# Regrouping HGRN2's short matrix products between the dense projections

## The chip, the core and the metric

The kernel runs on one core of one Trainium2 chip. The core's engines work beside each other, each on its own list of instructions in its own order: TensorE (PE in the profile; PEld is its loading of weights) multiplies matrices into the PSUM banks, VectorE (DVE) and ScalarE (ACT) do elementwise work, GpSimd (POOL) here mostly issues transfers, and SyncE (SP) issues the other transfers. Semaphores order work between engines. The metric is the device time of one execution in microseconds, lower is better. The median of three runs is 1842.91 us.

## The reference

A decoder trunk of two layers over 512 tokens and 1024 channels in float32. Each layer adds a half-step SwiGLU feed-forward, then three token mixers that share one normalised input and one output projection, then a second feed-forward. The part that matters is the HGRN2 mixer, a gated linear recurrence with 4 heads of 64 channels, computed in chunks of 64 tokens:

```python
bcum = jnp.cumsum(lfb, axis=-2)                       # lfb: log of the forget gate
rel = bcum[..., :, None, :] - bcum[..., None, :, :]
decay = jnp.where(causal, jnp.exp(jnp.where(causal, rel, 0.0)), 0.0)
scores = jnp.einsum('bhtd,bhsd,bhtsd->bhts', qb, kb, decay)
o = (jnp.einsum('bhts,bhsv->bhtv', scores, vb)
     + jnp.einsum('bhtd,bhdv->bhtv', qb * jnp.exp(bcum), state))
```

The decay depends on query token, key token and channel, so the scores of a chunk aren't one matrix product.

## The kernel before

The weights are streamed from memory. Each float32 weight tile is split into a high and a low part (a cast by ACT at line 301, a subtraction by DVE at line 302, into one of three `hl` buffers), and a dense product is three TensorE matmuls, high by high, high by low and low by high (lines 312, 318, 319). Python generators mix two kinds of work; the order in which they are recorded, turned into a list for each engine by a scheduler that knows their dependencies, is the order of execution on each engine.

In a layer's mixer stage `hgrn` (from line 1183 on) is such a generator, and the six dense projections of the attention group, `fox_qkv` (query, key and value of two halves, four steps each) are the other. After each part `hgrn` yields a number, and `mix` then records that many dense steps:

```python
for n in self.hgrn(l, hp, z, q, v, sg, og):
    for _ in range(n):
        next(dense, None)
```

One dense step is two weight tiles by four groups of 128 tokens by three matmuls: 24 matmuls of 128x256, all on TensorE. The 24 steps stand in the yields 1, 2, 4, 5, 5, 3, 3 and 1. A projection writes two PSUM banks, which ACT squares (line 1430), DVE reduces (line 1431) and DVE at last scales into the tile `qk` (line 1439) for the queries and keys; the value projections are split by lines 1447 and 1448. A later projection takes these banks again.

Between the dense steps `hgrn` puts bursts of short products, 64 rows by 64 columns of the array with 1, 32 or 64 columns moving through:

- line 1264: 32 products of keys and values, what each chunk adds to the recurrent state. ACT copies them out (line 1275), and DVE's scan over the chunks (line 1282) makes the states `S`.
- `scores` (line 1245): the scores in levels. A pair of query and key tokens belongs to the level of the highest bit in which their places in the chunk differ. For level l with half-width w = 2^(l-1), DVE makes the tile `e` from two half-width operations (lines 1332 and 1333), ACT takes its exponential, DVE multiplies its second halves by q into `e2` (line 1335), and 32 products of `e` and `e2` follow, 64x32 each. The diagonal (tile `e0`) and level 1 (tile `e1`) need only a sum over channels: 32 products each with a column of ones, one column wide.
- DVE writes each level into the score tile `A`: the diagonal at line 1287 by a multiplication, level 1 at line 1290 and the others at line 1344 by masked copies.
- `states` (line 1307): 28 products of `S` and the decayed queries, which ACT copies into `os` (lines 1315 and 1319).
- line 1360: 32 products of `A` and the values, the output.

Each of these float32 products shows as two matmul records in the profile, each with its own load of weights. The diagonal's and level 1's sums share two PSUM banks of tag `pt`; the levels' pairs take `pt`, `sc` and `pt` in turn; `states`, line 1264 and line 1360 take `sc`. Before the change the bursts of a layer are:

| burst | products | records | dense steps behind it |
|---|---|---|---|
| 1 | line 1264, sums of level 1, sums of the diagonal | 192 | 4 |
| 2 | levels 3 and 2, states | 184 | 5 |
| 3 | levels 5 and 4 | 128 | 5 |
| 4 | level 6 | 64 | 3 |
| 5 | output (line 1360) | 64 | 3 |

Of the kernel before, what the change touches and what calls it, by code (L numbers as in the profile page):

```python
# [23 lines left out]
P = 128  # L24
# [20 lines left out]
CH = 64  # L45
# [111 lines left out]
class Trunk:  # L157
# [1025 lines left out]
    def hgrn(self, l, hp, z, q, v, sg, og):  # L1183
        nc = self.nc
# [11 lines left out]
        h, t, n = tmp(), tmp(), tmp()  # L1196
# [44 lines left out]
        def scores(bank, at, held, moving, n):  # L1241
            for x in range(8):
                for hh, par in quarters:
                    c = 2 * x + par
                    nc.tensor.matmul(
                        bank[hh][rows[par], at + x * n : at + (x + 1) * n],
                        held[rows[hh], c * CH : (c + 1) * CH], moving(rows[hh], c),
                        start=True, stop=True,
                    )

        A = own("A", [P, 2, 8, CH])
        half = lambda a, w, i: a.rearrange("p (n two w) -> p n two w", two=2, w=w)[:, :, i, :]
        e0, e1 = tmp(), tmp()
# [6 lines left out]
        for x in range(8):  # L1260
            r, i = divmod(x, 4)
# [5 lines left out]
                    v[rows[par], i, f], start=True, stop=True,  # L1267
                )
        sb = [self.bank("pt") for _ in range(2)]
        for at, e in ((8, e1), (0, e0)):  # L1270
            scores(sb, at, e, lambda r, c: self.ones_c[r, :], 1)
        U, dec, S = tmp(), tmp(), own("S", [P, 2, HD, NCH])
        vc = lambda a: a.rearrange("p (r v c) -> p r v c", r=2, c=NCH)
        for par in range(2):
# [3 lines left out]
        for r in range(2):  # L1278
# [3 lines left out]
        nc.vector.tensor_tensor_scan(  # L1282
            S.rearrange("p r v c -> p (r v c)"), dec, U, 0.0, op0=ALU.mult, op1=ALU.add
        )
        for hh in range(2):
            d = lambda at, n: sb[hh][:, at : at + 8].unsqueeze(2).to_broadcast([P, 8, n])
            nc.vector.tensor_mul(
                A[:, hh], self.ident2.unsqueeze(1).to_broadcast([P, 8, CH]), d(0, CH)
            )
            nc.vector.copy_predicated(  # L1290
                A[:, hh, :, 1::2],
                self.lmask[:, 0, 1::2].unsqueeze(1).to_broadcast([P, 8, CH // 2]), d(8, CH // 2),
            )
        yield 4

# [4 lines left out]
        def states():  # L1300
            ob = [self.bank("sc") for _ in range(2)]
            for x in range(8):
                r, i = divmod(x, 4)
                for hh, par in quarters:
                    c = 2 * i + par
                    if c:
                        nc.tensor.matmul(
                            ob[hh][rows[par], x * CH : (x + 1) * CH], S[rows[hh], r, :, c - 1],
                            span(qe, r)[rows[hh], c * CH : (c + 1) * CH], start=True, stop=True,
                        )  # L1310
            for hh in range(2):
                for par in range(2):
                    out, src = chunk(os[rows[hh], :], par), C(ob[hh][rows[par], :])
                    if par:
                        nc.scalar.copy(out, src)
                    else:
                        for r in range(2):
                            x = slice(4 * r + 1, 4 * r + 4)
                            nc.scalar.copy(out[:, x, :], src[:, x, :])

        for group, then in (((2, 3), 5), ((4, 5), 5), ((6,), 3)):
            sb = [self.bank("pt" if group[0] != 4 else "sc") for _ in range(2)]
            made = []
            for at, lev in enumerate(group):
                w = 2**lev // 2
                e, e2 = tmp(), hp.tile([P, T], F32, tag=self.tt, name=self.n("e2"), bufs=self.tb)
                made.append((256 * at, lev, w, e, e2))
                n2 = W // (2 * w)
                ref = b.rearrange("p (n s) -> p n s", s=2 * w)[:, :, w - 1 : w].to_broadcast(
                    [P, n2, w]  # L1330
                )
                nc.vector.tensor_add(half(e, w, 0), half(kb, w, 0), ref)
                nc.vector.tensor_sub(half(e, w, 1), half(b, w, 1), ref)
                self.act(e, e, AF.Exp)
                nc.vector.tensor_mul(
                    e2.rearrange("p (n w) -> p n w", w=w), half(e, w, 1), half(q, w, 1)
                )
            for at, lev, w, e, e2 in made[::-1]:
                scores(sb, at, e, lambda r, c: e2[r, 32 * c : 32 * c + 32], 32)
            if group[0] == 2:  # L1340
                states()
            for at, lev, w, e, e2 in made[::-1]:
                for hh in range(2):
                    nc.vector.copy_predicated(
                        half(A[:, hh].rearrange("p x t -> p (x t)"), w, 1).rearrange(
                            "p (g n) w -> p g n w", g=8
                        ),
                        half(self.lmask[:, lev - 1, :], w, 1).unsqueeze(1).to_broadcast(
                            [P, 8, 32 // w, w]
                        ),  # L1350
                        sb[hh][:, at : at + 256].rearrange("p (g n w) -> p g n w", g=8, w=w),
                    )
            yield then

        ob = [self.bank("sc") for _ in range(2)]
        for x in range(8):
            r, i = divmod(x, 4)
# [6 lines left out]
        o, sq, r, t = tmp(), tmp(), tmp(), tmp()  # L1364
# [293 lines left out]
```

## Time and profile before

| | |
|---|---|
| median of three runs | 1842.91 us (1841.59 to 1846.96) |
| the profiled execution | 1837.37 us |
| its span, first to last instruction | 1835.6 us |
| PE, PEld, DVE, ACT, POOL busy | 99%, 92%, 79%, 54%, 9% |
| granted TensorE clock | 1.00 |
| the stage of bursts and dense steps, first layer | 401.5 to 481 us of the span |
| the same, second layer | 1306.9 to 1383 us |

All durations come from the one profiled execution, which was 5.5 us shorter than the median of the runs. An instruction's row has its start, its duration, the engine, the line of the kernel, what it writes and reads, its shape, and in brackets how long its engine stood idle before it and for what; "issue" means that the profile shows nothing it waited for. The ends of matmuls are modelled, and matmuls overlap: their starts tell the pace. An engine that is idle costs time only where PE comes to wait for it.

### The profile page before, as it was taken

How to read it: one execution, taken by the hardware profiler on the slowest of the kernel's cores; microseconds unless marked ns; L12 is line 12 of the kernel's file. 1: busy time of each engine (PE TensorE's matmuls, PEld its weight loads, DVE VectorE, ACT ScalarE, POOL GpSimd, SP SyncE). 2: the span in 40 equal slices, each digit the busy share in tenths (PEclk: the TensorE clock that was granted, in tenths of full speed). 3: DMA queues.
4: the chain of work that ended last, by engine and by line, in shares of the span. 5: the costliest groups of instructions: out<-in, count | busy, mean ns of one | idle time of the engine just before them, and what ended most of it. 6: DMA issues, size and time to landing. Idle time of an engine off the chain costs nothing.

```text
span 1835.6 us, 34734 instructions
## 1 busy us (share of the span) xinstructions
PE 1815.1 (99%) x14328; PEld 1685.2 (92%) x14328; DVE 1459.1 (79%) x2007; ACT 991.8 (54%) x1403; POOL 169.1 (9%) x168
## 2 busy tenths in 40 slices
PE   8999999999999999999999999999999999999999
PEld 6899999899878899999989999998997788999997
DVE  7888887676797888879668887875858878888883
ACT  4455555454675464555445555555547665555552
POOL 0011120100000001112001111201000000020210
PEclk9999999999999999999999999999999999999999
DMA  7659684232322766868266687813233228677762
GB/s 206 169 115 199 172 173 105 75 82 82 87 75 88 216 142 159 183 174 173 70 181 153 159 186 201 167 65 82 76 86 83 76 92 230 160 151 195 152 137 92
DMA packets 244782, 250.94 MB, mean 137 GB/s; under 512 B 19440, under 2 KB 229872, under 8 KB 244624
## 3 DMA queue, kind: packets, MB, share of 16 engines
q1 hardware_dynamic: 191024, 182.64, 32.5%
q0 software_dynamic: 53600, 66.09, 22.3%
q8 instruction: 112, 1.84, 0.4%
q14 instruction: 46, 0.38, 0.1%
HBM read 223.98 MB, written 2.10 MB: 123 GB/s over the span
## 4 chain that ended last, share of the span: by engine, by line
PE 89%; DVE 5%; ACT 3%; issue 1%; DMA 1%; SPq 1%; ACTq 0%
PE mm L312 13%; PE mm L319 13%; PE mm L318 13%; PE sc L319 6%; PE sc L318 6%; PE sc L312 6%; PE pt L312 6%; PE pt L318 6%; PE pt L319 6%; PE po L312 4%; PE po L318 4%; PE po L319 4%; DVE hl L302 1%; PE po L1510 1%; ACT hl L301 1%
## 5 line engine op out<-in xcount | busy, mean ns | idle before, releaser
L771 ACT CAST hl<-w 128x1024 fp32r<-128x1024 f32 x322 | 337.1, 1049 | 321.8 <-PE mm L319 79.0
L773 DVE TENSOR_TENSOR hl<-w,hl 128x1024 fp32r<-128x1024 f32 x322 | 392.8, 1222 | 86.8 <-ACT hl L771 86.6
L302 DVE TENSOR_TENSOR hl<-st,hl 128x512 fp32r<-128x512 f32 (+2 forms) x196 | 166.6, 853 | 119.3 <-ACT hl L301 118.0
L301 ACT CAST hl<-st 128x512 fp32r<-128x512 f32 (+2 forms) x196 | 146.4, 750 | 206.7 <-PE po L319 83.6
L312 PE MATMUL mm<-xc,hl 128*128 128x256 f32 (+1 forms) x732 | 201.5, 276 | 0.5 <-ACT g L882 0.5
L319 PE MATMUL mm<-xc,hl 128*128 128x256 f32 x728 | 201.4, 277 | 0.0
L318 PE MATMUL mm<-xc,hl 128*128 128x256 f32 x728 | 201.4, 277 | 0.0
L319 PE MATMUL sc<-xc,hl 128*128 128x256 f32 x528 | 146.6, 278 | 0.0
L312 PE MATMUL sc<-xc,hl 128*128 128x256 f32 (+1 forms) x530 | 146.6, 277 | 0.0
L318 PE MATMUL sc<-xc,hl 128*128 128x256 f32 x528 | 146.4, 277 | 0.0
L312 PEld LDWEIGHTS mm<-xc,hl 128*128 128x128 f32 x732 | 137.4, 188 | 0.9 <-ACT g L882 0.7
L319 PEld LDWEIGHTS mm<-xc,hl 128*128 128x128 f32 x728 | 136.7, 188 | 0.1
L318 PEld LDWEIGHTS mm<-xc,hl 128*128 128x128 f32 x728 | 136.7, 188 | 0.0
L312 PE MATMUL pt<-xc,hl 128*128 128x256 f32 (+1 forms) x484 | 133.4, 277 | 0.0
L318 PE MATMUL pt<-xc,hl 128*128 128x256 f32 x480 | 133.3, 278 | 0.0
L319 PE MATMUL pt<-xc,hl 128*128 128x256 f32 x480 | 133.0, 277 | 0.0
L312 PE MATMUL mm<-x,hl 128*128 128x512 f32 x272 | 108.9, 401 | 0.8 <-ACT cy L1158 0.8
L319 PE MATMUL mm<-x,hl 128*128 128x512 f32 x272 | 107.6, 395 | 0.0
L318 PE MATMUL mm<-x,hl 128*128 128x512 f32 x272 | 106.7, 392 | 0.0
L318 PEld LDWEIGHTS sc<-xc,hl 128*128 128x128 f32 x528 | 99.6, 189 | 0.0
L312 PEld LDWEIGHTS sc<-xc,hl 128*128 128x128 f32 x530 | 99.5, 188 | 0.2
L319 PEld LDWEIGHTS sc<-xc,hl 128*128 128x128 f32 x528 | 99.1, 188 | 0.1
(485 smaller groups left out, 5611.9 us busy)
## 6 DMA issues: line engine op xcount, KB each, us to landing
w<-in_ffn_w_in_dram SPq DMA_DIRECT2D x140, 512.0 KB
w<-in_ffn_w_out_dram SPq DMA_DIRECT2D x64, 512.0 KB
w<-in_ffn_w_out_dram POOLq DMA_DIRECT2D x56, 512.0 KB, 8.9
st<-in_w_mix_in_dram SPq DMA_DIRECT2D x88, 256.0 KB
st<-in_ffn_w_in_dram SPq DMA_DIRECT2D x72, 256.0 KB
w<-in_ffn_w_in_dram POOLq DMA_DIRECT2D x35, 512.0 KB, 8.4
w<-S POOLq DMA_DIRECT2D x35, 512.0 KB, 4.6
st<-in_ffn_w_out_dram SPq DMA_DIRECT2D x24, 512.0 KB
```

The costliest lines, as they stand in the source:

```text
L301: a = nc.scalar.copy(hi, src[:, c : c + w])
L302: b = nc.vector.tensor_sub(lo, src[:, c : c + w], hi)
L312: i = nc.tensor.matmul(acc[:, c], ah, bh[:, c], start=first and c.start == 0, stop=False, skip_group_check=True,)
L318: nc.tensor.matmul(acc, ah, bl, start=False, stop=False, skip_group_check=True)
L319: i = nc.tensor.matmul(acc, al, bh, start=False, stop=last, skip_group_check=True)
L771: A(nc.scalar.copy(hi, src))
L773: return lambda: V(nc.vector.tensor_sub(lo, src, hi))
L1510: nc.tensor.matmul(self.ob[:, t0 + u * P : t0 + 2 * P], V[:, j, h % 4].rearrange("p a d -> p (a d)"), part[:, j, u:, :].rearrange("p i t - ...
```

## The change

The 316 short products of a layer stay, and so do the 24 dense steps; their order changes. Level 1's sums move out of the first burst and follow level 2's products, into the same two banks (columns 256 to 263), and the masked copy of level 1 into `A` moves behind them. Levels 3 and 4 share a burst (banks `sc`), level 5 shares one with the states' products, level 6 stays alone. The yields become 1, 2, 4, 4, 4, 3, 2, 3 and 1, again 24.

| burst | products | records | dense steps behind it |
|---|---|---|---|
| 1 | line 1264, sums of the diagonal | 128 | 4 |
| 2 | level 2, sums of level 1 | 128 | 4 |
| 3 | levels 4 and 3 | 128 | 4 |
| 4 | level 5, states | 120 | 3 |
| 5 | level 6 | 64 | 2 |
| 6 | output | 64 | 3 |

On TensorE only the products of these stages move, and the whole list has one semaphore instruction more in each layer. On DVE and ACT the instructions of the stage change places among themselves; the lists of POOL and SP stay as they are.

```diff
         sb = [self.bank("pt") for _ in range(2)]
-        for at, e in ((8, e1), (0, e0)):
-            scores(sb, at, e, lambda r, c: self.ones_c[r, :], 1)
+        sums = lambda at, e: scores(sb, at, e, lambda r, c: self.ones_c[r, :], 1)
+        sums(0, e0)
...
+        d = lambda hh, at, n: sb[hh][:, at : at + 8].unsqueeze(2).to_broadcast([P, 8, n])
         for hh in range(2):
-            d = lambda at, n: sb[hh][:, at : at + 8].unsqueeze(2).to_broadcast([P, 8, n])
             nc.vector.tensor_mul(
-                A[:, hh], self.ident2.unsqueeze(1).to_broadcast([P, 8, CH]), d(0, CH)
-            )
-            nc.vector.copy_predicated(
-                A[:, hh, :, 1::2],
-                self.lmask[:, 0, 1::2].unsqueeze(1).to_broadcast([P, 8, CH // 2]), d(8, CH // 2),
+                A[:, hh], self.ident2.unsqueeze(1).to_broadcast([P, 8, CH]), d(hh, 0, CH)
             )
...
-        for group, then in (((2, 3), 5), ((4, 5), 5), ((6,), 3)):
-            sb = [self.bank("pt" if group[0] != 4 else "sc") for _ in range(2)]
+        for group, then in (((2,), 4), ((3, 4), 4), ((5,), 3), ((6,), 2)):
+            sb = [self.bank("pt" if group[0] != 3 else "sc") for _ in range(2)]
...
             if group[0] == 2:
+                sums(256, e1)
+                for hh in range(2):
+                    nc.vector.copy_predicated(
+                        A[:, hh, :, 1::2],
+                        self.lmask[:, 0, 1::2].unsqueeze(1).to_broadcast([P, 8, CH // 2]),
+                        d(hh, 256, CH // 2),
+                    )
+            if group[0] == 5:
                 states()
```

## The prediction

> **What bounds the kernel now.** I read the page's head first, then the waits of PE, then PE's instructions in order of time around HGRN2's short products, and last what DVE does there.
>
> ```profile
> span 1835.6 us, 34734 instructions
> PE 1815.1 (99%) x14328; PEld 1685.2 (92%) x14328; DVE 1459.1 (79%) x2007; ACT 991.8 (54%) x1403; POOL 169.1 (9%) x168
> q8 instruction: 112, 1.84, 0.4%
> PE 89%; DVE 5%; ACT 3%; issue 1%; DMA 1%; SPq 1%; ACTq 0%
> ```
>
> PE is busy 99% of the span and is 89% of the chain that ended last, so an edit counts here by what it does to PE: by work taken off it, or by idle time closed or opened. The third line is the queue that brings PE's instructions: 1.84 MB in 112 packets is 16.4 KB a packet, and 14328 matmuls with 14328 weight loads over 112 packets are 256 instructions a packet. A block of 256 instructions is thus 128 records of "load weights, multiply". PE's own waits, of which these are the two that lie in HGRN2:
>
> ```profile
> PE pt L1245 <- issue: 1.4, 1, 1.4
> PE sc L1307 <- issue: 1.3, 2, 0.7
> ```
>
> They wait for no engine ("issue"). Where they lie, PE in order of time (start, duration, the idle time in brackets), first layer and then second:
>
> ```profile
> 401.36 0.28 PE L319 MATMUL mm<-hl,x 128*128 128x256 f32 x1
> 401.57 1.16 PE L1264 MATMUL sc<-v,T 64*64 64x64 f32 x64
> 402.56 1.99 PE L1245 MATMUL pt<-ones_c,T 64*64 64x1 f32 x128
> 404.48 0.38 PE L312 MATMUL mm<-hl,x 128*128 128x256 f32 x1
> ...
> 415.98 2.07 PE L1245 MATMUL pt<-e,T 64*64 64x32 f32 x128
> 417.87 2.12 PE L1307 MATMUL sc<-z,S 64*64 64x64 f32 x52
> 420.72 0.46 PE L1307 MATMUL sc<-z,S 64*64 64x64 f32 x4 [0.73 <-issue]
> ...
> 434.92 2.07 PE L1245 MATMUL sc<-e,T 64*64 64x32 f32 x128
> 436.92 0.38 PE L312 MATMUL mm<-hl,x 128*128 128x256 f32 x1
> ...
> 450.53 0.28 PE L319 MATMUL mm<-hl,x 128*128 128x256 f32 x1
> 450.73 1.14 PE L1245 MATMUL pt<-e,T 64*64 64x32 f32 x64
> 451.80 0.38 PE L312 MATMUL mm<-hl,x 128*128 128x256 f32 x1
> ...
> 1306.74 0.28 PE L319 MATMUL mm<-hl,x 128*128 128x256 f32 x1
> 1306.95 1.16 PE L1264 MATMUL sc<-v,T 64*64 64x64 f32 x64
> 1307.93 1.80 PE L1245 MATMUL pt<-ones_c,T 64*64 64x1 f32 x113
> 1311.15 0.41 PE L1245 MATMUL pt<-ones_c,T 64*64 64x1 f32 x15 [1.42 <-issue]
> 1311.48 0.38 PE L312 MATMUL mm<-hl,x 128*128 128x256 f32 x1
> ...
> 1322.61 2.07 PE L1245 MATMUL pt<-e,T 64*64 64x32 f32 x128
> 1324.47 0.94 PE L1307 MATMUL sc<-z,S 64*64 64x64 f32 x16
> 1326.02 1.54 PE L1307 MATMUL sc<-z,S 64*64 64x64 f32 x40 [0.61 <-issue]
> ```
>
> The bursts of 192 and 184 records stop in the middle, the ones of 128 and 64 do not. The second layer's stops are one instruction block apart, twice: between them lie 15 short records, 96 dense ones and 144 short ones, as the count of this window says.
>
> ```profile
> 1311.10:1326.00 14.90, 14.26 (x255) 1.00 0.20 55
> ```
>
> 255 records are 510 instructions, with the two semaphore instructions between them 512, two blocks. So PE ran out of instructions. A record takes 1.85 us / 128 = 15 ns in a burst and 0.113 us in the dense stream; a block of short ones is used up in 2 us. How long a block takes to come is read backwards from the stops. The one at 1311.15 begins a block, so the block before began at record 177 - 128 = 49, at 1307.7: 3.4 us. For the one at 1326.02, record 16 of its burst, at 1322.85: 3.2 us; for 420.72, record 52, at 416.75: 4.0 us. A block that begins inside a burst must last 3.2 to 4.0 us; one that began in dense work costs nothing, since PE's sequencer is ahead there (the burst at 434.92 follows a boundary within 3 records, ran its 128 in 2 us and did not stop).
>
> The Trainium skill, page "Runtime: NRT & Kernel Launch", section "Instruction fetch mechanics", gives the same block of 256 instructions, but 2048 instructions of room on PE and a crossing that is "mostly hidden". By that rule no burst here would stop and the change would be worth only its extra burst. The stops two blocks apart speak against it; its case is the second rival.
>
> **The change part by part.** No product is added or dropped. Bursts were 192, 184, 128, 64, 64 records a layer, with 4, 5, 5 and 3 dense steps of 24 matmuls between; they become 128, 128, 128, 120, 64, 64 with 4, 4, 4, 3 and 2.
>
> *Stops.* PE ends are modelled, so a stop costs more than its idle: start to start it is the idle time plus the last record's modelled length, less 15 ns.
>
> ```profile
> L1307 PE MATMUL sc<-z,S x112: 213/280/331, 417.9 to 1327.3; 64*64 64x64 f32 x112
> ```
>
> That row should be read with its median, 0.28 us: 0.73 + 0.26 and 0.61 + 0.26. For the stop of 1.42 the two layers are compared: first burst from dense to dense 1311.48 - 1306.74 = 4.74 us against 404.48 - 401.36 = 3.12 us, 1.62 us. Together 0.99 + 0.87 + 1.62 = 3.5 us.
>
> Do they go? Counting 128 records from the stops through the new order (a semaphore shifts it by half a record), blocks begin at record 84, 116, 19 and 50 of the first four bursts of the first layer and at 49, 79, 110 and 13 in the second. Never two in a burst. The tightest is record 19 of 128: 109 short records (1.6 us), the way back into dense work (0.2) and 19 dense ones (2.2) give 4.0 us, where 3.2 to 4.0 are needed. Before, a block of 108 short and 20 dense (first layer, record 84 of 192) passed without a stop. The one at 13 holds the 56 states' products, which are slow (52 of them from 417.87 in some 2 us), and lasts over 5 us. So I take all 3.5 us; the bounds are 0 and 3.5.
>
> *One more burst a layer.* From its first record to the next dense matmul a burst of 128 takes 436.92 - 434.92 = 2.00 us and one of 64 takes 451.80 - 450.73 = 1.07, so 64 records are 0.93. From dense to dense the one of 64 takes 451.80 - 450.53 = 1.27; the rest, 0.34 less one ordinary spacing of 0.11, is the price of a burst: 0.23 us, 0.45 for both layers.
>
> *Spacing of the dense matmuls.* PE's matmuls in some windows (start and end, busy time, their count, the granted clock, DMA):
>
> ```profile
> 650.00:700.00 50.00, 50.00 (x435) 1.00 0.57 146
> 700.00:750.00 50.00, 50.00 (x427) 1.00 0.75 146
> 750.00:800.00 50.00, 50.00 (x428) 1.00 0.67 177
> 800.00:850.00 50.00, 50.00 (x444) 1.00 0.82 174
> ...
> 405.00:415.00 10.00, 10.00 (x87) 1.00 0.21 60
> 422.00:432.00 10.00, 10.00 (x91) 1.00 0.19 53
> 1312.00:1322.00 10.00, 10.00 (x90) 1.00 0.19 53
> ```
>
> At a granted clock of 1.00 the same matmuls run 444 or 427 to 50 us, 113 or 117 ns apart, each for long stretches. In the first layer's HGRN2 stage the wide spacing held between the first two bursts (87 against 91 in 10 us) and was gone after the second. No row says what a further burst does to it. From below: the wide stretch goes, some 140 matmuls by 4.5 ns, -0.6 us. From above: all 24 steps of both layers become wide, 1152 less 140 by 4.5 ns, +4.6 us. I take it to last until the burst with the states' products, which is two bursts (192 matmuls) later now: +0.9, and half of that as likely value, +0.4, since the bursts of 128 alone did not bring it on in the second layer.
>
> *DVE and ACT.* Same instructions, other order. DVE is the one to ask:
>
> ```profile
> 402.00:431.00 29.00, 26.19 (x50) 1.00 0.25 70
> 405.20 2.28 DVE L1282 TENSOR_TENSOR_SCAN S<-T,T 128x1024 f32<-128x1024 f32 x1
> 409.15 0.67 DVE L302 TENSOR_TENSOR hl<-st,hl 128x512 fp32r<-128x512 f32 x1
> 416.68 1.28 DVE L1439 TENSOR_TENSOR qk<-mm,fr 128x512 f32<-128x512 f32 x2
> 423.95 0.28 PE L312 MATMUL mm<-hl,x 128*128 128x256 f32 x1
> ```
>
> It is 90% full here. Four deadlines, from the new order of DVE with 0.6 us an instruction of this size. The second burst (about 414.9 in the first layer's times: 1.0 us less of first burst, then 96 matmuls) needs only level 2: two diagonals, its first half, the scan, two reductions, a weight half, four more: about 412, 3 us early. The third burst (about 428) needs level 4, done by about 418. A weight half is made some 3 us ahead of its use (the one at 409.15 serves the step that starts at 413), and none moves by more than 1 us relative to its step. The two scalings of the first projection's banks (416.68) end at about 417.1; PE needs these banks for the third projection, which began at 423.95 and now begins one burst and one step earlier, about 419.9: slack 2.7 us instead of 6. The level-1 write into A now waits for the second burst; it stands behind level 4, so DVE reaches it at about 418, after the burst's end at 417, and what is queued behind it (levels 5 and 6, the weight half for the step at 425) isn't held. ACT's states copies move to the fourth burst, with that burst's casts issued before them. POOL's and SP's instructions keep their order, so no transfer moves past another. All that costs nothing while the 2.7 us last; if they do not, each us beyond is PE's.
>
> *Sum.* -3.5 + 0.45 + 0.4 = -2.6 us. The profiled execution took 1837.37 us (span 1835.6), 5.5 below the median of the runs shown, 1842.91; so 1834.7 for an execution like it and **1840.3** against the median.
>
> **The rivals.** (1) *Faster by over 0.3%.* 0.3% is 5.5 us, about what a measurement of this kernel can tell from no change. The stops give 3.0 net; the rest must come from the spacing: against 444 the windows from 650 to 800 miss 9 + 17 + 16 = 42 matmuls, by 0.113 us 4.7 us. If PE comes out of the changed stage such that this stretch stays narrow, 1842.9 - 3.0 - 4.7 = 1835.2. For it: it is as large as needed. Against: that stretch lies far behind the edit. (2) *The change does not do what it says.* Blocks still come late, at the 4.0 us case in other bursts, or the stops had another cause: only the price of the bursts is left, 1843.4. The Trainium skill's hidden crossing, named above, gives the same time. (3) *Slower.* DVE takes the cover: if it falls behind by more than 2.7 us at the two scalings, PE stands before the third projection in each layer. From 6.8 us behind it decides: 2 x 4.1 - 2.6 = +5.6, 1848.5. For it: DVE's 90%. Against: its work is no more than before, and it has 6 us there now.
>
> **How the numbers follow.** Forecast 0.53, rival 2 0.14, rival 1 0.21, rival 3 0.12. The first two lie within 0.3%: same 0.67, faster 0.21, slower 0.12. Range: below, the forecast's 1840.3 less the spacing's 4.7 and another us of the runs' own spread (1841.59 to 1846.96), 1834; above, rival 2 with the stage's spacing at half its bound, 1843.4 + 2.3, and 1 us of spread, 1847.
>
> **What would show it.** Right: no "issue" wait of PE at the score and states lines (now three stops), six bursts a layer, from dense to dense 2.2 us for each of the first three; 87 or 90 matmuls in 10 us of this stage tell the spacing. Wrong: an "issue" stop inside the third burst of the first layer; a wait of PE for DVE's qk at the head of the third projection; DVE idle before the level-1 write into A; or wide spacing over the whole stage.

## The result, and the profile after

The changed kernel takes 1837.72 us (median of 22 runs, 1833.11 to 1844.9), the kernel before on the same chip 1843.72 us (22 runs, 1837.4 to 1853.28). The ratio is 0.9977 with a 95% interval of 0.9966 to 0.9988: 4.2 us less (2.2 to 6.3), where 2.6 us less were forecast. The change is real and smaller than the spread of either kernel's own runs.

The profiled execution shows this only in part. The head of its page:

```profile
span 1839.6 us, 34732 instructions
PE 1820.4 (99%) x14328; PEld 1690.6 (92%) x14328; DVE 1459.1 (79%) x2007; ACT 991.5 (54%) x1403; POOL 169.0 (9%) x168
```

It took 1841.40 us, 4.0 us more than the profiled execution before, although the median fell by 6.0. PE is busy 99% in both, so the difference must lie in how fast PE goes, not in waits. The waits of PE (total, times, longest, in us), the largest and the only one that is still put down to "issue":

```profile
PE mm L1608 <- DMA xs<-in_x_dram: 6.9, 2, 3.8
...
PE sc L1493 <- issue: 0.5, 2, 0.3
```

The first stands at the kernel's start, the second in the attention stage. The two rows of HGRN2's "issue" waits, three stops, are gone. PE in order of time (start, duration, tiles, count) around the first four bursts of the first layer, and bursts 1 and 4 of the second:

```profile
402.86 1.16 PE L1264 MATMUL sc<-v,T 64*64 64x64 f32 x64
403.84 1.06 PE L1245 MATMUL pt<-ones_c,T 64*64 64x1 f32 x64
404.83 0.38 PE L312 MATMUL mm<-hl,x 128*128 128x256 f32 x1
...
416.33 1.14 PE L1245 MATMUL pt<-e,T 64*64 64x32 f32 x64
417.29 1.09 PE L1245 MATMUL pt<-ones_c,T 64*64 64x1 f32 x64
...
429.20 0.28 PE L319 MATMUL mm<-hl,x 128*128 128x256 f32 x1
429.40 2.07 PE L1245 MATMUL sc<-e,T 64*64 64x32 f32 x128
431.40 0.38 PE L312 MATMUL mm<-hl,x 128*128 128x256 f32 x1
...
442.29 0.28 PE L319 MATMUL po<-hl,x 128*128 128x256 f32 x1
442.50 1.14 PE L1245 MATMUL pt<-e,T 64*64 64x32 f32 x64
443.45 2.13 PE L1303 MATMUL sc<-z,S 64*64 64x64 f32 x56
445.50 0.39 PE L312 MATMUL mm<-hl,x 128*128 128x256 f32 x1
...
1307.67 1.16 PE L1264 MATMUL sc<-v,T 64*64 64x64 f32 x64
1308.65 1.07 PE L1245 MATMUL pt<-ones_c,T 64*64 64x1 f32 x64
...
1348.13 1.13 PE L1245 MATMUL pt<-e,T 64*64 64x32 f32 x64
1349.08 2.12 PE L1303 MATMUL sc<-z,S 64*64 64x64 f32 x56
1351.14 0.39 PE L312 MATMUL mm<-hl,x 128*128 128x256 f32 x1
```

No row is cut in two any more. From dense to dense the bursts take 2.18, 2.18, 2.20 (431.40 - 429.20), 3.22, 1.27 and 1.30 us in both layers. For a sum I take off each burst the one ordinary spacing of 0.113 us that would stand there without it: before, the ten bursts come to 26.74 us, now the twelve come to 23.36. The bursts gave 3.4 us, as they should.

What took it back in this execution is the pace of the dense matmuls. PE's matmuls by window (start:end, busy, their count, granted clock, DMA share, GB/s), after:

```profile
700.00:750.00 50.00, 50.00 (x443) 1.00 0.79 156
1010.00:1060.00 50.00, 50.00 (x427) 1.00 0.71 166
1600.00:1650.00 50.00, 50.00 (x427) 1.00 0.75 153
405.00:415.00 10.00, 10.00 (x86) 1.00 0.21 55
432.00:442.00 10.00, 10.00 (x91) 1.00 0.34 93
1310.00:1320.00 10.00, 10.00 (x87) 1.00 0.22 56
```

The same two windows far behind the edit, before:

```profile
1010.00:1060.00 50.00, 50.00 (x443) 1.00 0.73 167
1600.00:1650.00 50.00, 50.00 (x444) 1.00 0.77 161
```

The stretch from 681 to 797 us, wide in the profile before, is narrow now, but two others of the same length are wide: some 983 matmuls each, from 1007 us and from 1587 us. Each wide matmul is 4.5 ns slower (118 against 113), so such a stretch costs 4.4 us. Summed over all dense matmuls, the wide spacing cost 6.4 us before and 12.1 after: +5.7. With the bursts' -3.4, a first matmul on split weights 0.9 us later (10.23 against 9.30 us into the span) and a rest of +0.8 that I can't place, that is the 4 us by which this profiled execution is longer. Whether the change causes the wide stretches, one profile can't tell; the runs below do.

### The profile page after: what moved, and what is told of

Same layout as the page of the kernel before. It is cut to its first block, busy times and chain, and to the rows that moved or that the text cites. A ratio compares the mean times of both kernels' runs of the same rounds, so it can differ in the third digit from the quotient of the medians.

```text
span 1839.6 us, 34732 instructions
## 1 busy us (share of the span) xinstructions
PE 1820.4 (99%) x14328; PEld 1690.6 (92%) x14328; DVE 1459.1 (79%) x2007; ACT 991.5 (54%) x1403; POOL 169.0 (9%) x168
## 4 chain that ended last, share of the span: by engine, by line
PE 90%; DVE 5%; ACT 3%; issue 1%; DMA 1%; SPq 0%; ACTq 0%
PE mm L312 13%; PE mm L319 13%; PE mm L318 13%; PE sc L312 6%; PE sc L318 6%; PE sc L319 6%; PE pt L312 6%; PE pt L318 6%; PE pt L319 6%; PE po L312 4%; PE po L318 4%; PE po L319 4%; DVE hl L302 1%; PE po L1514 1%; PE pt L1245 1%
```

## The experiments

Two questions. Were the stops due to instruction blocks that come late, so that the blocks' position in the list is what counts (my theory), or to the make of the large bursts or to something that merely went along with the regrouping? And are the wide stretches an effect of the change, or of the single execution? In all that follows, a burst's time is read from PE's matmul starts as above, and "sum of bursts" is that for both layers together. The last column is the granted TensorE clock, mean of the runs in the second.

| run | time, us (runs) | ratio to before on the same chip | sum of bursts, us | excess by wide spacing, us | clock |
|---|---|---|---|---|---|
| before | 1843.72 (22) | | 26.74 | 6.4 | see below |
| after | 1837.72 (22) | 0.9977 [0.9966, 0.9988] | 23.36 | 12.1 | 1.0000 |
| before_shifted82 | 1836.69 (12) | 0.9979 [0.9965, 0.9993] | 22.99 | 4.6 | 0.9998 |
| after_again | 1835.51 (12) | 0.9979 [0.9962, 0.9996] | 23.34 | 3.6 | 1.0000 |
| after_reset | 1833.29 (7) | 0.9953 [0.9932, 0.9973] | 23.34 | 4.1 | 1.0000 |
| after_shifted82 | 1835.62 (1) | | 23.43 | 4.4 | 1.000 |
| before_shifted30 | 1843.6 (1) | | 26.73 | 4.4 | 0.997 |
| sums_in_first | 1843.88 (1) | | 25.14 | 11.7 | 0.999 |
| two_more_bursts | 1834.06 (1) | | 24.41 | 3.3 | 1.000 |
| before_reset | 1839.92 (11) | 1.0009 [1.0, 1.0019] | 26.64 | 5.7 | 0.9986 |
| after_reset_chunk1 | 1834.14 (11) | 0.9954 [0.9939, 0.9968] | 23.35 | 5.5 | 1.0000 |
| after_third | 1837.75 (12) | 0.997 [0.9954, 0.9987] | 23.35 | 10.4 | 0.9999 |
| shift_and_reset | 1838.2 (12) | 0.9976 [0.9962, 0.9989] | 22.98 | 4.2 | 0.9997 |

Before_shifted82 to after_shifted82 ran on one chip (before there: 1839.16 us, mean clock 0.9987 in 24 runs), before_shifted30 to before_reset on another (1837.21 us, 0.9989 in 15), the last three on a third (1842.55 us, 0.9985 in 28), so only ratios compare across them. The single times of before_shifted30 and sums_in_first can't be told from the spread of single runs and are not compared; their bursts are what they were run for. The lower clock goes with the stops: every kernel that has them shows it, and the others have 0.9997 or more. What it costs is said under before_shifted30.

### before_shifted82: the old bursts, other block boundaries

```diff
+        pad = self.bank("po")
+        for _ in range(41):
+            nc.tensor.matmul(
+                pad[:64, :1], self.ident[:64, :64], self.ident[:64, :1], start=True, stop=True
+            )
```

The kernel before, with 41 products that nobody reads at the program's start. They are 82 records, so every boundary between two blocks lies 82 records earlier in every burst, and nothing else of the stage changes. (Line numbers are 5 higher in this kernel.)

> The kernel before, with 41 tiny products (82 records) put at its very start, where TensorE waits for its first data; nothing else differs. It moves the places where an instruction block of 128 records begins by 82 records: to records 3 and 131 and to 98 in the first two bursts of the first layer, to 95 and 62 in those of the second. Theory of the late blocks: the three stops (3.5 us) vanish although the bursts are still 192 and 184 long; from dense to dense the ten bursts sum to 23.3 us, less one spacing each, instead of 26.7 (at most 0.3 more, if the block that begins at record 13 of the second layer's third burst comes late); against the kernel before the ratio is about 0.998, and as there is no extra burst it is as fast as the changed kernel or 0.4 us faster. Rival, that regrouping helps by the order it gives to VectorE and ScalarE or by shorter bursts as such: the stops and the time of the kernel before stay.

PE in order of time, end of the first layer's second burst and start of the second layer's first:

```profile
419.12 2.07 PE L1250 MATMUL pt<-e,T 64*64 64x32 f32 x128
421.01 2.12 PE L1312 MATMUL sc<-z,S 64*64 64x64 f32 x56
423.06 0.39 PE L317 MATMUL mm<-hl,x 128*128 128x256 f32 x1
...
1306.22 1.16 PE L1269 MATMUL sc<-v,T 64*64 64x64 f32 x64
1307.20 1.99 PE L1250 MATMUL pt<-ones_c,T 64*64 64x1 f32 x128
```

All 56 states' products and all 128 sums run through: the same bursts of 192 and 184 records, and no stop. The first layer's first burst holds two boundaries even here, at records 3 and 131, and runs through as well; so two boundaries in one burst are not enough for a stop. The four large ones take 3.12, 4.15, 3.11 and 4.19 us. The sum falls from 26.74 to 22.99, so the three stops were worth 3.75 us. And against the changed kernel's 23.34 the old bursts without stops are 0.35 us cheaper: two bursts fewer, 0.18 us each.

What it costs is the start. The first matmul on split weights of this kernel, and, in a second fence, of the changed one (after_again):

```profile
13.68 0.78 PE L317 MATMUL sc<-x,hl 128*128 128x512 f32 x1
```

```profile
9.94 0.78 PE L312 MATMUL sc<-x,hl 128*128 128x512 f32 x1
```

3.7 us later, of which about 2 are left at the first burst (404.71 us here; 402.72 in the profile of after_again). This is a likely reason why a kernel with the cheapest bursts of all, expected as fast as the changed one or 0.4 us faster, only has its ratio, 0.9979.

### after_again: the changed kernel once more

No edit.

> The changed kernel itself, beside the others on one chip. Late blocks: bursts from dense to dense sum to 23.4 us in any execution, no stop. Spacing: the excess of the wide spacing in the dense stream of this execution differs from the 12 us of the first one by steps of some 4.5 us, and the time with it. Ratio to the kernel before 0.997 to 0.999.

The bursts repeat to 0.02 us (23.34). The spacing does not. PE's matmuls in the windows of above:

```profile
1010.00:1060.00 50.00, 50.00 (x444) 1.00 0.74 167
1600.00:1650.00 50.00, 50.00 (x444) 1.00 0.79 156
405.00:415.00 10.00, 10.00 (x87) 1.00 0.23 57
```

444 where the first profile of the same kernel had 427. No stretch of 980 is wide here; the excess is 3.6 us instead of 12.1 and the span 1831.1 us instead of 1839.6: 8.5 us less of the one, 8.5 us less of the other. The long stretches thus differ between executions of one kernel. Over the eleven profiles without the later split, 2 of 16 feed-forwards of the kernels with the old bursts held one, and 6 of 28 of those with new ones: too few to show a share of the change in it, or to rule one out. The window from 405 is wide in both executions, as it was before.

### after_reset and before_reset: a split matmul against the wide spacing, in the wrong place

```diff
-                kind == "I" and p == "P1" and w in (covered, *(f0 for f0, _ in CHUNKS)),
+                kind == "I" and (
+                    p == "P1" and w in (covered, *(f0 for f0, _ in CHUNKS))
+                    or p == "P6" and w == covered
+                ),
```

The wide stretches end where the kernel has a matmul of 256 columns as two of 128. The edit puts one more such split into each feed-forward, on the changed kernel and on the one before.

> The changed kernel, with the first matmul of the third product (P6) of each feed-forward's first streamed unit split into two of 128 columns, as it is already done for the first product of each chunk (four splits more in all). In both traces the wide spacing (117 instead of 113 ns) begins at the second product of such a unit, if it begins, and ends at the next split matmul some 115 us later. Theory of the spacing: wide stretches there are cut to under 4 us, the excess in the feed-forwards falls from 4 to 12 us an execution to under 1 us, at a price of 0.13 us a split; the time is 4 to 5 us (0.25%) below the changed kernel's median and the runs lie closer together. Rival, that the spacing is set by something else (data traffic, the clock): wide stretches last as long as before, and the time is the changed kernel's plus 0.5 us.

> The kernel before with the split of the third product's first matmul in each feed-forward's first streamed unit, as in the changed kernel with it. Theory of the spacing: it is independent of the bursts, so the split is worth the same here: no wide stretch of 982 matmuls (4.4 us), time 2 to 5 us below the kernel before, ratio 0.997 to 0.999, with the three stops (26.7 us of bursts) still there. Rival, that the gain of the split on the changed kernel was chance: ratio 1.000 to 1.001.

After_reset came out at 0.9953 (0.9932 to 0.9973), and no feed-forward of its profile held a long wide stretch. Before_reset came out at 1.0009 (1.0 to 1.0019), and one of its feed-forwards was wide from 1008.5 to 1124.3 us, 983 matmuls. The reason lies in the edit: `covered` is the first streamed unit, and the split came 30 to 40 us ahead of the point where the stretches begin, so it could end none. The good ratio of after_reset can't be the split's work by that mechanism; its interval overlaps that of after_again, so it need not be an effect at all. The old bursts in before_reset still have their stops (26.64), at records 179, 174 and 141 where they had been at 180, 177 and 144. The new splits put one record more ahead of the first layer's bursts and three ahead of the second's, so the stops moved by the count here too, though no one had meant them to. The last of them is the shortest of all, 0.52 us from start to start.

### after_shifted82: the changed kernel with the shift

The edit of before_shifted82, on the changed kernel.

> The changed kernel with the same 82 records ahead. Late blocks: with at most 128 records a burst no place of the blocks should matter; blocks now begin at records 3, 34, 65, 96 of the first layer's first four bursts and 94, 126, 28, 59 of the second's; no stop, from dense to dense the twelve bursts sum to 23.4 us as before the shift. Rival, that the changed kernel escapes the stops by the luck of its places alone: a stop of 0.5 us or more in one of the bursts, most likely where a block begins early in a burst (34 of the first layer's second, 28 of the second layer's third).

The sum is 23.43 us, against 23.34 without the shift; 0.09 us of it is in the second layer's second burst. The same shift that takes 3.75 us off the old bursts does nothing for the new: they have no stop to lose, and moving the blocks brings none.

### before_shifted30: stops at places named beforehand

The same edit with 15 products, 30 records. Boundaries 30 records earlier leave two of them in three of the four large bursts, and only one in the second layer's second.

> The kernel before with 15 tiny products (30 records) at its start instead of 41. Blocks now begin at records 55 and 183 of the first burst and 22 and 150 of the second in the first layer, at 19 and 147 of the first and 114 of the second in the second layer. Theory of the late blocks: three stops again, but at other records than before: at 183 and 150 in the first layer (the first of them in a burst that had none) and at 147 in the second layer's first burst, of 0.9 to 1.6 us from start to start; none in the second layer's second burst, which had one. Bursts sum to 26 to 27 us. Rival, that the stops belong to the products (the states' products, the sums) and not to the count: they stay at 180, 177 and 144, or vanish.

PE in order of time, where it stood (idle time in brackets):

```profile
406.26 1.87 PE L1250 MATMUL pt<-ones_c,T 64*64 64x1 f32 x119
409.30 0.33 PE L1250 MATMUL pt<-ones_c,T 64*64 64x1 f32 x9 [1.17 <-issue]
...
424.18 0.92 PE L1312 MATMUL sc<-z,S 64*64 64x64 f32 x22
426.30 1.43 PE L1312 MATMUL sc<-z,S 64*64 64x64 f32 x34 [1.20 <-issue]
...
1312.47 1.39 PE L1250 MATMUL pt<-ones_c,T 64*64 64x1 f32 x83
1314.56 0.89 PE L1250 MATMUL pt<-ones_c,T 64*64 64x1 f32 x45 [0.70 <-issue]
```

The stops came at record 64 + 119 = 183, at 128 + 22 = 150 and at 64 + 83 = 147, where they had been at none, 180 and 177. The second layer's second burst, which stopped at record 144, ran through. The first layer's first burst, which did not stop in the profile before, now does: its boundary at record 85 moved to 55, and the next came in at 183. This is the run that decides for the blocks: one and the same order of products stops or doesn't, by where the list is cut. Counted through PE's whole list, semaphores included, the ten stops of the four kernels that have any (before, before_shifted30, sums_in_first, before_reset) lie whole multiples of 256 instructions apart, to within one instruction.

The trace also shows the blocks on their way. For each of the ten, one packet of 16 KB of the instruction queue (q8) starts 0.0 to 1.8 us after the block before began, and PE goes on 1.2 to 1.6 us after the packet's end; in the second layer's first burst of before it ran from 1308.80 to 1309.75 us, and PE went on at 1311.15. (Which block a packet holds the trace doesn't say.) The two bursts that held two boundaries and ran through, those at records 3 and 131 (before_shifted82) and 2 and 130 (shift_and_reset), had that packet start 1.4 and 1.5 us before PE reached the first boundary, while dense work still ran; it ended 2.1 and 2.4 us before PE reached the second.

A stop has a second price, which my theory didn't have. The granted clock halves shortly after it: PE's matmuls in the three stretches of 3.41 us in which the profile of before_shifted30 has it at 0.50, and in one as long right behind the first of them (start:end, busy, count, granted clock, DMA share, GB/s):

```profile
410.75:414.16 3.41, 3.41 (x19) 0.50 0.00 0
427.82:431.23 3.41, 3.41 (x17) 0.50 0.00 0
1315.28:1318.69 3.41, 3.41 (x24) 0.50 0.02 5
414.16:417.57 3.41, 3.41 (x32) 1.00 0.25 68
```

They begin 0.7 to 1.5 us after the three stops end. Dense matmuls are 214 ns apart there instead of 113 or 118, which costs 1.5 to 1.6 us a stretch, as much as the stop itself. It does not follow every stop: the profile before had three stops and none, sums_in_first one after its one stop, before_reset a double one of 6.83 us around the end of one of its three stops. That is five of ten. Between their first 20 and their last 3 us the nine profiles without stops have one such stretch in all, in after_third at 47.82 us, right after a wait of PE for DVE of 1.81 us. By the mean clocks (0.9987, 0.9989 and 0.9985 before, 0.9999 to 1.0000 after; one such stretch is 0.0009 of the span) an execution of the kernel before has 1.2 to 1.6 of them, and the changed kernel hardly any: an estimate of some 2 us beyond the bursts' 3.4.

### sums_in_first: half of the change undone

```diff
         sums = lambda at, e: scores(sb, at, e, lambda r, c: self.ones_c[r, :], 1)
+        sums(8, e1)
         sums(0, e0)
...
+            nc.vector.copy_predicated(
+                A[:, hh, :, 1::2],
+                self.lmask[:, 0, 1::2].unsqueeze(1).to_broadcast([P, 8, CH // 2]),
+                d(hh, 8, CH // 2),
+            )
...
-            if group[0] == 2:
-                sums(256, e1)
```

The changed kernel with level 1's sums back in the first burst (192, 64, 128, 120, 64 and 64 records). The masked copies move with the sums.

> One part of the change alone: the levels regrouped (2; 4 and 3; 5 with the states; 6), but level 1's sums left in the first burst, which is 192 records again, and the second 64. Late blocks: the stops in the second bursts are gone, the one at record 176 of the second layer's first burst stays, 1.6 us; the first layer's first burst (a block begins at 85 only) has none. Twelve bursts sum to 23.4 + 1.6 = 25.0 us. Rival, that the grouping of the levels does it all: no stop.

The second layer's first burst, PE in order of time:

```profile
1312.52 1.77 PE L1245 MATMUL pt<-ones_c,T 64*64 64x1 f32 x112
1315.84 0.41 PE L1245 MATMUL pt<-ones_c,T 64*64 64x1 f32 x16 [1.55 <-issue]
```

One stop, at record 176, of 1.74 us from start to start, and none in the first layer's, though it has 192 records too. The sum is 25.14, 1.8 above the changed kernel's. So, with the blocks where they lay, moving the sums removed the one stop, and regrouping the levels the other two.

### two_more_bursts: the price of a burst

```diff
+        yield 1
         sums(0, e0)
...
-        yield 4
+        yield 3
...
-        for group, then in (((2,), 4), ((3, 4), 4), ((5,), 3), ((6,), 2)):
+        for group, then in (((2,), 4), ((3, 4), 3), ((5,), 3), ((6,), 2)):
...
                 scores(sb, at, e, lambda r, c: e2[r, 32 * c : 32 * c + 32], 32)
+                if lev == 4:
+                    yield 1
```

The changed kernel with bursts 1 and 3 cut in two by a dense step: four bursts more in all.

> The changed kernel with one dense step drawn between the states' increments (line 1264) and the diagonal's sums, and one between levels 4 and 3: eight bursts a layer, 16 in all, none over 120 records, dense steps still 24. This doses the price of a burst: by the rows of before 0.23 us each, by the shifted kernel against the changed one 0.18 us. The sum of the bursts from dense to dense, less one spacing each, goes from 23.34 to 24.1 to 24.3 us; no stop. Rival, that an extra burst also costs waits of TensorE for VectorE: a wait for e or the weight halves in the stage, and over 1 us more.

The sum is 24.41, a little above what was expected, and no wait of PE for another engine was added in the stage: 1.07 us more for four bursts, 0.27 each (0.11 of the 1.07 are in the fourth burst of the first layer, 3.33 instead of 3.22). With 0.18 from the comparison above, a burst's price is 0.18 to 0.27 us.

### after_reset_chunk1: the split where the wide stretches begin

```diff
-                    or p == "P6" and w == covered
+                    or p == "P6" and w == CHUNKS[1][0]
```

The edit of after_reset, with the split right behind the product in which the long stretches begin.

> The changed kernel with the first matmul of the third product (P6) split in two in the first unit of the second chunk of each feed-forward (four splits more in all). The earlier pair had the split in the first streamed unit, about 30 us too early: in all traces the stretches of 982 matmuls begin at the second product of this later unit. Theory, that a split matmul ends the wide spacing: no stretch of 982 any more, at most one product (24 matmuls, 0.1 us) is wide there, stretches of about 193 and 235 elsewhere stay; the slower executions (4.4 us each stretch) go, and the median is 1 to 5 us below the changed kernel's on this chip. Rival, that the stretch goes on through the split: stretches of 982 in some feed-forwards, time that of the changed kernel plus 0.5 us.

On this chip the changed kernel took 1837.75 us and this one 1834.14 (1831.72 to 1837.2), with 0.9954 against 0.997 to the kernel before. No feed-forward of its profile held a long wide stretch. In the last but one the split can be seen at work, PE in order of time, where the row of 128 columns is the split:

```profile
1586.25 0.28 PE L319 MATMUL pt<-xc,hl 128*128 128x256 f32 x1
1586.37 0.33 PE L312 MATMUL pt<-xc,hl 128*128 128x128 f32 x2
1586.54 0.33 PE L318 MATMUL pt<-xc,hl 128*128 128x256 f32 x1
...
1586.94 0.28 PE L318 MATMUL pt<-xc,hl 128*128 128x256 f32 x1
1587.05 0.28 PE L319 MATMUL pt<-xc,hl 128*128 128x256 f32 x1
```

Starts are 0.12 apart ahead of it (23 matmuls from 1583.7 us), 0.11 behind it. Counting the profiles without a split there, 8 of 44 feed-forwards held a stretch of some 983 wide matmuls; with it, 0 of 8 here and in shift_and_reset. That is what one expects by chance 2 times in 10 ((36/44)^8 = 0.20), and the intervals of 0.9954 and 0.997 overlap, so the advantage over the changed kernel, 3.6 us by the medians, is likely and not established. It is the fastest of the kernels on its chip.

### after_third: the changed kernel, beside it

No edit.

> The changed kernel once more beside the other two: bursts sum to 23.4 us without a stop; ratio to the kernel before 0.997 to 0.999; executions in steps of about 4.4 us by how many stretches of 982 they hold.

0.997 (0.9954 to 0.9987), and a profile with two wide stretches of 983 matmuls, from 682.8 and from 1012.7 us. The first is the one that the profile before had and the first profile of after had not. Three profiles of one kernel held 2, 0 and 2 long stretches. The expected steps of 4.4 us can't be made out in the times of its twelve executions, which lie between 1833.56 and 1842.13 us without clear gaps.

### shift_and_reset: no regrouping at all

The kernel before, with the 41 products of before_shifted82 and the split of after_reset_chunk1.

> The kernel before with its old bursts, 82 records ahead and the split in the second chunk's first unit: both causes taken away without regrouping. No stop, bursts sum to 23.0 us (two bursts fewer than the changed kernel), no stretch of 982. If the two causes are all there is, it is 0 to 1 us faster than the changed kernel with the split, ratio to the kernel before 0.995 to 0.998. If regrouping had worth of its own, it is slower than that kernel.

The bursts are the cheapest again, 22.98 us, but the time is 1838.2 (1835.43 to 1840.76), 0.9976 (0.9962 to 0.9989), some 4 us behind after_reset_chunk1 on the same chip, where 0 to 1 us ahead was expected. About 2 of them may be the padding's, less 0.4 that the bursts are cheaper; some 2 us stay open, which is no more than the two intervals leave. So this run doesn't settle whether regrouping has a worth of its own beyond the stops.

## Why the prediction was right, and where its working was off

**The bound** was read rightly: PE at 99%, and the three stops were a part of PE's time that an order could remove.

**The stops** (3.5 forecast). Their cause, blocks of 256 instructions that come late, is shown by the shifts and by the packets of q8: the stops go at 82 records, come back at the records worked out for 30, and one stays where half the change is undone. Their size in the bursts is 3.75 us (26.74 - 22.99). From start to start the three take 1.01, 1.61 and 0.89, together 3.51; of the other 0.24, 0.17 are in the first layer's second burst (5.33 against 4.15 us). That all three would go held in every profile of the changed order; the tightest block, which I had at 4.0 us, lasted 3.8 to 3.9.

The rule behind it was too simple. Already before the change only three of the four bursts of 192 and 184 records stopped. I had a block that begins inside a burst need 3.2 to 4.0 us. Over the ten stops the next block began 2.6 to 4.1 us after it, and blocks that began at record 2 or 3 of a burst cost nothing after 1.9 us. How deep in the burst a block begins counts: at record 13 the stop was 0.52 us, at 16 and 19 it was 0.9, deeper 1.0 to 1.7. Record 19 of the changed order, the case I called tight, thus had some 1.1 us to spare against the stop at record 19 in before_shifted30 (2.77 us).

The Trainium skill, page "Runtime: NRT & Kernel Launch", section "Instruction fetch mechanics", has the crossing from block to block mostly hidden; by that rule the second rival, no change but the bursts' price, should have held. The runs decide against it: the 192 records of before_shifted30's first burst lost 1.36 us at their second crossing. Where only one boundary fell into one of HGRN2's bursts, or the first of two fell at record 2 or 3, no run shows an idle time at it, as the rule says.

**One more burst a layer** (0.45). Measured 0.18 each from one comparison and 0.27 from the other; 0.23 lies between. Right.

**Spacing** (+0.4, bounds -0.6 and +4.6). This step failed, in mechanism more than in sum. I took the wide spacing of the first layer's stage to last two bursts longer; it ended at the second burst as before (140 matmuls against 141). In the second layer, for which I expected none, it held from 1310 to 1347.9 us in the first profile, some 281 matmuls or 1.3 us, up to the very burst with the states' products at which I had it end in the first layer; after_again has no such stretch. So the term is 0 to 1.3 us by execution. What I didn't see is that the spacing outside the stage is no constant: I treated the profile before, with its one long stretch, as the state to compare with, and a long stretch is 4.4 us, as much as the change is worth.

**The clock** (no term). I took the granted clock of 1.00 from the one profile before and asked no further. In that profile none of the three stops was followed by half clock; in the kernel's runs on average it was, and the stops' second price, some 2 us by the estimate above, is missing from the sum.

**DVE and ACT** (nothing, with 2.7 us of slack at the third projection). DVE's scaling, its masked copy of level 1, and PE's third projection after the change:

```profile
416.94 1.29 DVE L1443 TENSOR_TENSOR qk<-mm,fr 128x512 f32<-128x512 f32 x2
419.35 1.31 DVE L1339 COPY_PREDICATED A<-lmask,pt 128x256 f32<-128x256 uint8 x2
...
421.15 0.28 PE L312 MATMUL mm<-hl,x 128*128 128x256 f32 x1
```

The second scaling ended at 418.2. I had 417.1 for a first burst at 401.57; it began 1.3 us later, so the forecast is 418.4. PE came at 421.15: slack 2.9 us. The copy at 419.35 follows the second burst's end (about 418.3), and nothing on PE waited for what is queued behind it.

**The rivals.** The first had the right sign and a wrong mechanism: the stretch from 681 us did stay narrow, as it asked, but two others came, and in after_third it was wide again. No run shows that the regrouping sets it. The second falls with the shifts, the third with the slack. The change is faster by 0.23%, within the 0.3% that the forecast's case named.

**The sum.** Bursts account for 3.4 us, the clock by the estimate for some 2 more; the three comparisons of the changed kernel gave 4.2, 3.9 and 5.5 us. Each interval holds 3.4 and 5.4, so the times alone can't tell the two; the traces and the clocks speak for the larger. The same account fits the shift of 82 records: 3.75 us of stops and some 2 of clock, less about 2 for the padding, against the 3.9 us that its ratio gives. The forecast of 2.6 lies inside each interval as well, towards the lower end, since it lacked the clock; with intervals of 4 to 6 us that is no proof of its sum.

## What to carry to other kernels

Count instructions as well as time: where an engine runs short instructions faster than its list arrives, a burst should not contain the start of two blocks unless the first comes within its first few records, and a stop shows as an "issue" wait that moves with the block boundary. Look at the granted clock right behind such a stop, in more than one execution: the price there was as large as the stop. Test it by shifting the whole list with a few dummy instructions; that tells it from every cause in the data in one run, though the dummies have a price of their own. When a change is worth less than the kernel's own spread, find what makes the spread before reading the two profiles against each other, since here the profile of the faster kernel was the longer one.

## What the runs showed of the hardware

Dense matmuls of 256 columns run 113 or 118 ns apart at the same granted clock of 1.00, and stay so for stretches of some twenty to 983 matmuls; 427 against 444 matmuls in 50 us is the same work of the same kernel in two executions. A long stretch begins in the second product of a feed-forward's second chunk, after a short hiccup at a semaphore, and ended each time at the next matmul that is split into 128 columns. It costs 4.4 us, and in the profiles between none and two occur, a large part of a spread of some 10 us between executions. What PE does differently in the two no view here shows.

The list of PE comes in blocks of 256 instructions, one packet of 16 KB each. When a block of 128 records of 15 ns began at record 13 or deeper of a burst and the next in the same burst, PE stopped for 0.5 to 1.7 us from start to start (ten of ten); when it began at record 2 or 3, not at all (two of two). Five of the ten stops, of 0.7 to 1.6 us of idle time, came with 3.41 us or more at a granted clock of 0.50, in which dense matmuls ran some 214 ns apart. And of the short products the states' are much the slowest, 56 records in 2.05 us (443.45 to the next dense matmul at 445.50), more than twice the 15 ns of the others.
